# Gated recurrence of a two-block model: each level's exponents in two VectorE instructions, none of the stage's arithmetic on GpSimd

## The chip, the cores and the metric

One Trainium2 chip, one of its cores, one launch. The metric is the device time of the whole program in microseconds. The engines of the core are called by the names of the profile: PE (TensorE), ACT (ScalarE), DVE (VectorE), POOL (GpSimd), SP (SyncE, which issues most DMAs). Each engine takes its instructions in the order in which they stand in its queue.

## What is computed

Two blocks of a model on 512 tokens of width 1024. The first mixes tokens by a gated recurrence in both directions and by attention, and then has a mixture of 16 experts; the second has sparse attention, a short convolution and a feed-forward layer. The change lies in the recurrence of the first block, which has 4 heads of 128 channels:

```python
def hgrn_gates(f_pre, lb):
    f_pre = heads(f_pre.astype(jnp.float32), HG_HEADS)
    lb = lb.reshape(HG_HEADS, HG_DK)
    log_f = jnp.log(lb + (1 - lb) * jax.nn.sigmoid(f_pre))
    key = (1 - lb) * jax.nn.sigmoid(-f_pre)
    return key, log_f

def hgrn_chunk_scan(q, k, v, log_f, s0):
    """S_t = diag(f_t) S_{t-1} + k_t v_t^T, o_t = S_t^T q_t."""
    ...
        cum = jnp.cumsum(fc, axis=2)
        rel = jnp.where(incl, cum[:, :, :, None, :] - cum[:, :, None, :, :], -jnp.inf)
        scores = jnp.einsum("bhtk,bhsk,bhtsk->bhts", qc, kc, jnp.exp(rel))
    ...

def hgrn_bidir(q, i, k_f, lf_f, k_b, lf_b, s_f0, s_b0):
    o_f, s_f = hgrn_chunk_scan(q, k_f, i, lf_f, s_f0)
    flip = lambda a: a[:, ::-1]
    o_b, s_b = hgrn_chunk_scan(flip(q), flip(k_b), flip(i), flip(lf_b), s_b0)
    return o_f + flip(o_b), s_f, s_b
```

## The kernel before, in words

Channels lie on the partitions and the 512 tokens along the free axis. `first_mixer` runs `ctx_part` (the context's keys, values and states), then `hgrn` (the recurrence), `attention`, `merge_b`, `mix_out`, `router`, `moe`; then come `second_mixer` and `ffn`.

`hgrn` alternates two pieces of code for heads 0 to 3. `gates(h)` multiplies the activations by four blocks of 128 columns of the input weights (forget gates forward and backward, queries, output gate), 24 matmuls of 128x512 a block (L84 to L86, three for each 128 rows, since weights and activations are split into a high and a low part; ACT makes the high part at L76, DVE the low part at L78). It then takes a sigmoid (L564), a logarithm (L569) and the output gate `gr` (L572 to L575). `hgrn_head` takes the running sums of the logarithms in both directions (the scans of L610 and L611), subtracts the logarithm of the keys (L619), and then goes through seven levels, from blocks of 128 tokens down to blocks of 2 (L641 to L663). At each level the pairs of tokens that lie in the two halves of one block get their scores from one product: queries and keys are scaled by exponentials of the distance of their sums to the sum at the middle of the block. The tile `D` holds the exponents, `D[:, 0]` for queries and `D[:, 1]` for keys. L650 and L651 (DVE) write the query half, forward and backward direction apart, L652 and L653 (POOL) the key half; L654 (ACT) takes the exponential of both, L655 (DVE) multiplies by the queries, and L627 (PE) makes the scores, in `fs` for the two upper levels and in `lv` for the five lower ones, which DVE merges by a predicated copy (L663).

After the levels come the states: ACT makes the decayed keys (L675, L676), PE transposes them (`kt`, L685) and multiplies by the values (`sp`, L690), DVE chains the three states of a direction (`S`, L693) from the context's state, which POOL copies in at L678 and L679. PE then makes the head's output `po` (L702 to L704), ACT squares it (L708), PE sums over channels (`pr`, L711), and DVE and ACT apply the norm and the gate. Behind head 3, `hgrn` ends with twelve blocks of 24 matmuls of 128x256 that give keys, values and queries of the attention.

The program text doesn't give the order on the engines. A scheduler places all instructions by its own estimate of their times and keeps the data dependencies, so the matmuls of `gates(h + 1)` stand on PE in among those of `hgrn_head(h)`, and an instruction that takes another time in that estimate moves others. A tile's buffer is reused when everything that read its last contents is done (`D` has 4, `lv` 2, `S` and `Q` 1).

Of the kernel before, what the change touches and what calls it, by code (L numbers as in the profile page):

```python
# [13 lines left out]
AF = mybir.ActivationFunctionType  # L14
# [48 lines left out]

class Build:
# [26 lines left out]
    def wT(self, w, c0, n):  # L91
        """Yields (hi, lo) [128, 8, 128] for each 128 columns of w[:, c0:c0+n]."""
# [12 lines left out]
    def wN(self, w, c0, n):  # L105
        """Yields for each 256 columns the list over k of (hi, lo) [128, 256]."""
        w3 = w.rearrange("(k p) f -> p k f", p=128)
        K = w3.shape[1]
        for c in range(c0, c0 + n, 256):
            m = min(256, c0 + n - c)  # L110
            t = self.wload(w3[:, :, c:c + m], [128, K, m])
            ks = []
            for k in range(0, K, 4):
                h, l = self.split(t[:, k:k + 4, :], [128, 4, m])
                ks += [(h[:, i], l[:, i]) for i in range(4)]
            yield ks

    def gemmT(self, wh, wl, xh, xl, n0, n1):
        """out^T block: weights stationary, tokens n0:n1 moving."""
# [7 lines left out]
    def gemmN(self, ks, xh, xl, b, ps=None):  # L127
        """token block b of out: activations stationary, weights moving."""
# [9 lines left out]
    def rstd(self, pool, out, ss, scale, n):  # L138
        """out = 1/sqrt(ss*scale + eps) on [128, n]"""
# [38 lines left out]
    def first_mixer(self):  # L178
# [18 lines left out]
        at = 0  # L197
# [51 lines left out]
        # row statistics and transposes of x and ctx  # L249
# [25 lines left out]
        # scale and shift of the first norm by 256 columns, each pair followed by the activations' chunks  # L275
        wm3 = I["w_mod"][0].rearrange("(k p) f -> p k f", p=128)
        # mod[:, which, i, k]: shift (0), scale (1) for x (i=0) and ctx (i=1)
# [56 lines left out]
        def rest(i):  # L334
            """the last chunks of x, behind the first weights"""
# [68 lines left out]
    def ctx_part(self, cx, rest):  # L404
# [7 lines left out]
        # f gates of the context  # L412
# [8 lines left out]
        # shift and scale of the second norm by halves, each behind step i of what follows  # L421
# [9 lines left out]
        # i (values), tokens on partitions  # L431
# [8 lines left out]
        # keys and values of the attention: the context's  # L440
# [67 lines left out]
    def rope(self, pool, out, x, which, b, nh):  # L508
        """out = rope(x * gain): x [128, nh*64]"""
# [13 lines left out]
    def hgrn(self):  # L523
# [22 lines left out]
        def gates(h):  # L546
# [19 lines left out]
            # ln(key) stands in for key: it joins the exponents  # L566
# [4 lines left out]
            # gr / (1 + exp(-gr)); below -40, where the exponential nears the logarithm's bound, gr * exp(-40)  # L571
# [3 lines left out]
            nc.gpsimd.tensor_tensor(gr, sg, gr, op=ALU.mult)  # L575
# [7 lines left out]
        # keys, values and queries of the attention  # L583
# [12 lines left out]
    def table(self, name):  # L596
        """loads the activation tables of that name behind what was issued so far"""
        return self.tc.keep_in_program_order(self.nc.scalar.preload_act_table_set(name))

    def after(self, ins, first):  # L600
        """ins is issued behind first (the same engine)"""
# [4 lines left out]
    def hgrn_head(self, hp, pp, h, q, K, CU, sg):  # L606
# [5 lines left out]
        # P[s, t] for 4 blocks of 128 tokens; C holds its blocks of 32 on the diagonal  # L612
# [4 lines left out]
        nc.gpsimd.tensor_tensor(KS, kf, kb, op=ALU.add)  # L617
# [4 lines left out]
        def scores(out, kk, qq, m, x):  # L622
            """out[s, b, t'] for parts of m tokens: the part of t is that of s, x flipped"""
# [17 lines left out]
        for l in range(6, -1, -1):  # L641
# [4 lines left out]
            vw = lambda t: t.rearrange("p (n two h) -> p n two h", two=2, h=H)  # L646
            Dq, Dk, F, Bk, Fk, Bl = (vw(t) for t in (D[:, 0], D[:, 1], cf, cb, lf, lb))
            mf = F[:, :, 0, H - 1:H].to_broadcast([128, n, H])
            mb = Bk[:, :, 1, 0:1].to_broadcast([128, n, H])
            nc.vector.tensor_tensor(Dq[:, :, 1], F[:, :, 1], mf, op=ALU.subtract)  # L650
            nc.vector.tensor_tensor(Dq[:, :, 0], Bk[:, :, 0], mb, op=ALU.subtract)  # L651
            nc.gpsimd.tensor_tensor(Dk[:, :, 0], mf, Fk[:, :, 0], op=ALU.subtract)  # L652
            nc.gpsimd.tensor_tensor(Dk[:, :, 1], mb, Bl[:, :, 1], op=ALU.subtract)  # L653
# [14 lines left out]
        # chunk states  # L668
# [9 lines left out]
        nc.gpsimd.tensor_copy(S[:, 0, 0], self.S0[:, h, 0])  # L678
        nc.gpsimd.tensor_copy(S[:, 1, 3], self.S0[:, h, 1])  # L679
# [25 lines left out]
        # norm over the head's channels, gain, gate  # L705
# [13 lines left out]
    def attention(self):  # L719
# [4 lines left out]
        # keys: norm, rope, transpose, split; both halves of the partitions hold a copy  # L724
# [5 lines left out]
        # rope tables with the gains folded in: [which, block, cos|sin, 64]  # L730
# [32 lines left out]
        for n in range(2):  # L763
# [6 lines left out]
            # the norm of q and the softmax scale enter as the exponent's scale  # L770
# [54 lines left out]
    def gated(self, w_gate, c0, w_br, act, j, done):  # L825
        """done(j, sigmoid(gate block j), branch block j in PSUM) for two blocks of 128"""
# [42 lines left out]
    def mod_rows(self, pool, psp, wi, tag, halves=(0, 1)):  # L869
        """yields for halves of w_mod columns wi*1024..: rows 32j hold partial products of c"""  # L870
# [14 lines left out]
    def mod_bc(self, pool, psp, out, wi, tag, half):  # L885
        """a half of out [128, 1024]: that part of the modulation, the same on every partition; returns its end"""
# [13 lines left out]
    def mod_col(self, pool, psp, out, wi, half, tag="mr"):  # L900
        """half of out [128, 8]: that part of the modulation, by chunks of 128 on the partitions"""
# [10 lines left out]
    def mix_out(self, end):  # L912
        """X += g1 * y by groups of 256 columns, each followed into the router's logits"""
# [43 lines left out]
    def router(self):  # L957
        """aff: softmax of the logits; sl: the place (from 1) of a token among an expert's chosen, or 0"""
# [23 lines left out]
        # the 64 largest become -1  # L982
# [16 lines left out]
    def moe(self):  # L999
# [3 lines left out]
        # the first weights also fill places that are needed later  # L1003
# [6 lines left out]
        def mload(src, last):  # L1010
            if last == 2 and not self.tail:
                # the last product's: places that nothing else waits for
# [24 lines left out]
        def gemm_parts(ps, lhs, wa, wb):  # L1037
            """by parts of the columns"""
# [611 lines left out]
```

## Time and profile before

| | |
|---|---|
| median of three runs | 1845.2 us (1839.9 to 1847.11) |
| the profiled execution, first to last instruction | 1847.6 us |
| recurrence with the projections behind it, 131.0 to 330.5 us | 199.5 us |
| PE busy over the span | 1740.2 us (94%) |
| DVE busy over the span | 847.1 us (46%) |
| ACT busy over the span | 634.8 us (34%) |
| POOL busy over the span | 199.7 us (11%) |
| mean granted clock of PE | 0.969 |

The profiled execution is one more run than the three. Its record gives the span alone, 1847.6 us, which lies 2.4 us over the median. In the rows below, times are microseconds from the start of the span; a granted clock of 1.00 is 2.4 GHz and one of 0.50 is 1.2 GHz.

### The profile page before, as it was taken

The numbers are of one execution on the slowest core, as the hardware profiler recorded it, in microseconds if no ns is written. First come the engines' busy times: TensorE is split into PE (matmuls) and PEld (weight loads), VectorE is DVE, ScalarE is ACT, GpSimd is POOL, SyncE is SP. The second block draws the span as 40 slices with busy tenths as digits, with TensorE's granted clock in tenths as the row PEclk, the third lists the DMA queues.
The fourth block names the chain that finished last, engine by engine and source line by source line (L and its number), as shares of the span: only waits on it lengthen the run. The fifth ranks groups of instructions, "written<-read, shape, count | busy, mean of one in ns | idle before, by whom it ended". The sixth has DMA issues, their size and how long they took to land.

```text
span 1847.6 us, 27736 instructions
## 1 busy us (share of the span) xinstructions
PE 1740.2 (94%) x11511; PEld 1273.8 (69%) x11511; DVE 847.1 (46%) x1615; ACT 634.8 (34%) x1106; POOL 199.7 (11%) x231
## 2 busy tenths in 40 slices
PE   5998888999999599999999998899999999999999
PEld 2986668777778553444434433797677989898989
DVE  5637897865334512221221222656675553434342
ACT  4627674556333210010000100555463242313231
POOL 0103342122110000000000020500221000000000
PEclk9999898999999799999999999898899999999999
DMA  9562111201568578999999996341001222233231
GB/s 304 179 207 70 47 47 55 77 15 35 201 219 299 189 296 325 404 409 381 386 380 367 397 396 205 103 160 46 24 24 48 91 92 91 93 92 105 78 114 47
DMA packets 177398, 327.81 MB, mean 177 GB/s; under 512 B 8580, under 2 KB 115816, under 8 KB 177272
## 3 DMA queue, kind: packets, MB, share of 16 engines
q1 hardware_dynamic: 176480, 325.44, 49.0%
q8 instruction: 91, 1.49, 0.3%
q10 hardware_dynamic: 744, 0.51, 0.1%
q14 instruction: 35, 0.29, 0.1%
q0 software_dynamic: 48, 0.08, 0.0%
HBM read 323.91 MB, written 2.10 MB: 176 GB/s over the span
## 4 chain that ended last, share of the span: by engine, by line
PE 63%; DVE 4%; ACT 1%; issue 1%; DMA 1%; SPq 0%; ACTq 0%; DVEq 0%
PE mm L85 10%; PE mm L84 10%; PE mm L86 10%; PE G L1058 7%; PE U L1058 6%; PE Y L1058 5%; PE mm L1080 3%; PE po L1582 2%; PE mm L1153 1%; PE pt L1543 1%; PE sc L1522 1%; PE Y L1046 1%; PE mm L1154 1%; PE sc L1523 1%; PE hp L1445 0%
## 5 line engine op out<-in xcount | busy, mean ns | idle before, releaser
L76 ACT ACTIVATE whi<-wraw 128x1024 fp32r<-128x1024 f32 (+1 forms) x171 | 173.5, 1018 | 376.4 <-PE mm L85 177.9
L78 DVE TENSOR_TENSOR wlo<-wraw,whi 128x1024 fp32r<-128x1024 f32 (+1 forms) x171 | 207.2, 1213 | 125.7 <-ACT whi L76 125.3
L85 PE MATMUL mm<-whi,ul 128*128 128x256 f32 x512 | 144.3, 282 | 0.0
L86 PE MATMUL mm<-whi,uh 128*128 128x256 f32 x512 | 143.2, 281 | 0.0
L84 PE MATMUL mm<-wlo,uh 128*128 128x256 f32 x512 | 143.2, 281 | 0.0
L84 PE MATMUL mm<-HXl,whi 128*128 128x512 f32 x256 | 106.1, 415 | 0.0
L85 PE MATMUL mm<-HXh,wlo 128*128 128x512 f32 x256 | 105.9, 414 | 0.1
L86 PE MATMUL mm<-HXh,whi 128*128 128x512 f32 x256 | 105.2, 411 | 0.0
L84 PE MATMUL mm<-H,whi 128*128 128x512 f32 x256 | 99.7, 390 | 0.0
L85 PE MATMUL mm<-H,wlo 128*128 128x512 f32 x256 | 99.6, 389 | 0.0
L86 PE MATMUL mm<-H,whi 128*128 128x512 f32 x256 | 99.6, 389 | 0.0
L85 PEld LDWEIGHTS mm<-whi,ul 128*128 128x128 f32 x512 | 96.5, 188 | 1.0 <-DVE ul L1613 0.8
L84 PEld LDWEIGHTS mm<-wlo,uh 128*128 128x128 f32 x512 | 96.2, 188 | 0.2
L86 PEld LDWEIGHTS mm<-whi,uh 128*128 128x128 f32 x512 | 96.2, 188 | 0.0
L1080 PEld LDWEIGHTS mm<-D,X 128*128 128x128 f32 x512 | 61.9, 199 | 18.5 <-issue 15.4
L1622 DVE SCALAR_TENSOR_TENSOR X<-mm,r,X 128x256 f32<-128x256 f32 x64 | 30.9, 483 | 88.2 <-PE mm L86 88.2
L1080 PE MATMUL mm<-D,X 128*128 128x128 f32 x512 | 66.8, 288 | 2.8 <-DVE D L1075 1.8
L1146 POOL TENSOR_TENSOR X<-X,acc 128x1024 f32<-128x1024 f32 x4 | 9.3, 2369 | 534.7 <-issue 534.7
L1123 DVE TENSOR_TENSOR hy<-hy,U 128x1024 f32<-128x1024 f32 x8 | 9.8, 1222 | 124.4 <-PE U L1058 124.4
L1058 PE MATMUL Y<-mwt,xh 128*64 128x512 f32 x240 | 59.9, 594 | 5.4 <-DVE xh L1126 5.4
L1608 DVE TENSOR_SCALAR r<-mm 128x512 f32<-128x512 f32 x32 | 22.1, 691 | 85.2 <-PE mm L86 85.2
L1148 DVE SCALAR_TENSOR_TENSOR hy<-Y,gc,g 128x512 f32<-128x512 f32 (+1 forms) x17 | 11.6, 715 | 106.2 <-PE Y L1058 100.2
(541 smaller groups left out, 4238.9 us busy)
## 6 DMA issues: line engine op xcount, KB each, us to landing
mwt<-in_w_exp_gate_dram SPq DMA_DIRECT2D x41, 1024.0 KB, 8.3
mwt<-in_w_exp_up_dram SPq DMA_DIRECT2D x35, 1024.0 KB, 10.4
mwt<-in_w_exp_down_dram SPq DMA_DIRECT2D x33, 1024.0 KB, 11.9
wraw<-in_w_in_dram SPq DMA_DIRECT2D x29, 1024.0 KB, 5.3
wraw<-in_w_mod_dram SPq DMA_DIRECT2D x16, 1024.0 KB, 6.9
wraw<-in_w_up_dram SPq DMA_DIRECT2D x16, 1024.0 KB, 5.7
wraw<-in_w_down_dram SPq DMA_DIRECT2D x16, 1024.0 KB, 5.3
mwh<-in_w_exp_up_dram SPq DMA_DIRECT2D x30, 512.0 KB, 8.7
```

The lines of the kernel that those rows point to most:

```text
L76: i1 = self.nc.scalar.activation(hi, src, AF.Copy)
L78: i2 = self.nc.vector.tensor_tensor(lo, src, hi, op=ALU.subtract)
L84: mm(ps, ah, bl, start=first, stop=False)
L85: mm(ps, al, bh, start=False, stop=False)
L86: mm(ps, ah, bh, start=False, stop=last)
L1046: nc.tensor.matmul(y[64 * a:64 * a + 64], lhs[:, k, 64 * a:64 * a + 64], tl[a][k4], start=(k == 0), stop=(k == 7))
L1058: nc.tensor.matmul(ps[64 * a:64 * a + 64, n], lhs[:, k, 64 * a:64 * a + 64], tl[a][k2][:, n * 512:(n + 1) * 512], start=(k == 0), stop=(k ...
L1080: nc.tensor.matmul(ps, self.X[:, b, k * 128:(k + 1) * 128], Ds[:, b], start=(b == 0), stop=(b == 3))
L1153: nc.tensor.matmul(ps, oh[:, b * 128:(b + 1) * 128], yh[:, 1, s], start=True, stop=False)
L1582: nc.tensor.matmul(po[64 * j:64 * j + 64], lh, rh, start=(i == 0), stop=(i == len(items) - 1))
L1608: nc.vector.tensor_scalar(r, ps, 0.0, None, op0=ALU.max)
L1622: nc.vector.scalar_tensor_tensor(self.X[:, b, s], ps, r2[:, b:b + 1], self.X[:, b, s], op0=ALU.mult, op1=ALU.add)
```

## The change

The two DVE instructions of a level that write the query half become one, and the two POOL instructions that write the key half become one on DVE. A new helper `view` builds access patterns by hand: the new first axis of length 2 is the direction, and its step leads from the second half of a block in the forward sums to the first half in the backward sums (and the other way for keys). Besides, the product for `gr`, the sum of the keys `KS` move from POOL to DVE, and the two copies of the context's state move from POOL to ACT. The rest of the difference between the two programs is comments and docstrings, which are removed. Line numbers in the changed program are 5 higher up to the levels and 3 higher behind them.

```diff
+def view(t, at, dims):
+    return bass.AP(t.tensor, t.offset + at, [list(t.ap[0])] + dims)
...
-            nc.gpsimd.tensor_tensor(gr, sg, gr, op=ALU.mult)
+            nc.vector.tensor_tensor(gr, sg, gr, op=ALU.mult)
...
-        nc.gpsimd.tensor_tensor(KS, kf, kb, op=ALU.add)
+        nc.vector.tensor_tensor(KS, kf, kb, op=ALU.add)
...
             D = hp.tile([128, 2, 512], F32, name="D", tag="D", bufs=4)
-            vw = lambda t: t.rearrange("p (n two h) -> p n two h", two=2, h=H)
-            Dq, Dk, F, Bk, Fk, Bl = (vw(t) for t in (D[:, 0], D[:, 1], cf, cb, lf, lb))
-            mf = F[:, :, 0, H - 1:H].to_broadcast([128, n, H])
-            mb = Bk[:, :, 1, 0:1].to_broadcast([128, n, H])
-            nc.vector.tensor_tensor(Dq[:, :, 1], F[:, :, 1], mf, op=ALU.subtract)
-            nc.vector.tensor_tensor(Dq[:, :, 0], Bk[:, :, 0], mb, op=ALU.subtract)
-            nc.gpsimd.tensor_tensor(Dk[:, :, 0], mf, Fk[:, :, 0], op=ALU.subtract)
-            nc.gpsimd.tensor_tensor(Dk[:, :, 1], mb, Bl[:, :, 1], op=ALU.subtract)
+            late = lambda t: view(t, H, [[512 - H, 2], [B, n], [1, H]])
+            early = lambda t: view(t, 0, [[512 + H, 2], [B, n], [1, H]])
+            mid = view(CU, H - 1, [[513, 2], [B, n], [0, H]])
+            nc.vector.tensor_tensor(view(D, H, [[-H, 2], [B, n], [1, H]]), late(CU), mid, op=ALU.subtract)
+            nc.vector.tensor_tensor(view(D, 512, [[H, 2], [B, n], [1, H]]), mid, early(KL), op=ALU.subtract)
             nc.scalar.activation(D, D, AF.Exp)
...
-        nc.gpsimd.tensor_copy(S[:, 0, 0], self.S0[:, h, 0])
-        nc.gpsimd.tensor_copy(S[:, 1, 3], self.S0[:, h, 1])
+        nc.scalar.activation(S[:, 0, 0], self.S0[:, h, 0], AF.Copy)
+        nc.scalar.activation(S[:, 1, 3], self.S0[:, h, 1], AF.Copy)
```

The scheduler answers with another order, at two places above all. The first is PE in the lower levels of head 0. `lv<-D` and `fs<-D` are the scores of a level, `kt` and `sp` belong to the states, `po` to the head's output; `mm` are the products of the next head's gates. Before:

```order
L627 MATMUL lv<-D 32x32 x16
L86 MATMUL mm<-HXh,whi 128x512
L685 MATMUL kt<-ca,D 128x128
L84 MATMUL mm<-HXl,whi 128x512
L85 MATMUL mm<-HXh,wlo 128x512
L685 MATMUL kt<-ca,D 128x128
L86 MATMUL mm<-HXh,whi 128x512
L84 MATMUL mm<-HXl,whi 128x512
L85 MATMUL mm<-HXh,wlo 128x512
L627 MATMUL lv<-D 32x32 x16
L86 MATMUL mm<-HXh,whi 128x512
L690 MATMUL sp<-V,kn 128x128 x3
```

and now:

```order
L632 MATMUL lv<-D 32x32 x48
L688 MATMUL kt<-ca,D 128x128
L632 MATMUL lv<-D 32x32 x16
L688 MATMUL kt<-ca,D 128x128 x2
L693 MATMUL sp<-V,kn 128x128 x3
L632 MATMUL lv<-D 32x32 x16
L688 MATMUL kt<-ca,D 128x128 x3
L705 MATMUL po<-P,V 128x128
L706 MATMUL po<-Q,S 128x128
L693 MATMUL sp<-V,kn 128x128 x3
L89 MATMUL mm<-HXl,whi 128x512
```

Before, matmuls of the next head's gates stand between the levels down to the last: 30 of them from the first `fs<-D` of head 0 to its last `lv<-D`, 23 in head 1, 29 in head 2. Now there are 8 in head 0, 10 each in heads 1 and 2 and none in head 3; from the first `lv<-D` to the second `sp` not one is left, 16 stand between that and the rest of `po`, and the last three of the next head's second gate stand behind `pr`.

The second place is DVE at the end of head 0, where `D<-D,q` is the last levels' multiplication by the queries, `C` the merged lower levels, `S` the states and `wlo` the low part of a block of weights. Before:

```order
L78 TENSOR_TENSOR wlo<-wraw,whi 128x1024
L663 COPY_PREDICATED C<-lev,lv 128x128
L655 TENSOR_TENSOR D<-D,q 128x512
L78 TENSOR_TENSOR wlo<-wraw,whi 128x1024
L663 COPY_PREDICATED C<-lev,lv 128x128
L693 SCALAR_TENSOR_TENSOR S<-S,dec,sp 128x128
L666 COPY P<-C 32x4x32 x4
```

and now:

```order
L658 TENSOR_TENSOR D<-D,q 128x512
L561 TENSOR_SCALAR R<-mm 128x512
L696 SCALAR_TENSOR_TENSOR S<-S,dec,sp 128x128
L666 COPY_PREDICATED C<-lev,lv 128x128
L696 SCALAR_TENSOR_TENSOR S<-S,dec,sp 128x128
L669 COPY P<-C 32x4x32 x4
L696 SCALAR_TENSOR_TENSOR S<-S,dec,sp 128x128
L83 TENSOR_TENSOR wlo<-wraw,whi 128x1024
L696 SCALAR_TENSOR_TENSOR S<-S,dec,sp 128x128
L83 TENSOR_TENSOR wlo<-wraw,whi 128x1024
```

The low parts of the weights, which stood among the levels, now stand between the steps of the second direction's states, three of them there in all, and every head from 0 to 2 has this same order.

## Rows read from the trace of the kernel before

**Rows 1.** The page, part 1: busy time by engine.

```profile
span 1847.6 us, 27736 instructions
PE 1740.2 (94%) x11511; PEld 1273.8 (69%) x11511; DVE 847.1 (46%) x1615; ACT 634.8 (34%) x1106; POOL 199.7 (11%) x231
```

**Rows 2.** Busy time by stretch: from:to, length, busy (instructions), granted clock, DMA.

```profile
131.00:330.50 199.50, 178.24 (x1937) 146.29 (x1936) 162.22 (x285) 125.44 (x184) 72.87 (x81) 0.91 0.20 59
330.50:570.00 239.50, 235.80 (x1425) 178.58 (x1423) 126.76 (x244) 117.06 (x200) 45.08 (x44) 1.00 0.34 115
```

**Rows 3.** Timeline, DVE: the forward scan of each head (start, took, instruction, idle before).

```profile
149.85 1.23 DVE L610 TENSOR_TENSOR_SCAN R<-seg,R 128x512 f32<-128x512 f32 x1 [2.71 <-ACT R L569]
...
184.15 1.71 DVE L610 TENSOR_TENSOR_SCAN R<-seg,R 128x512 f32<-128x512 f32 x1 [0.78 <-ACT R L569]
...
231.87 1.23 DVE L610 TENSOR_TENSOR_SCAN R<-seg,R 128x512 f32<-128x512 f32 x1 [1.81 <-ACT R L569]
...
266.18 1.71 DVE L610 TENSOR_TENSOR_SCAN R<-seg,R 128x512 f32<-128x512 f32 x1 [0.78 <-ACT R L569]
```

**Rows 4.** Timeline, PE: the last two projections behind the recurrence.

```profile
330.23 0.28 PE L85 MATMUL mm<-whi,HXl 128*128 128x256 f32 x1
330.35 0.28 PE L86 MATMUL mm<-whi,HXh 128*128 128x256 f32 x1
```

**Rows 5.** Timeline of head 0's upper levels, DVE and, below, POOL.

```profile
155.72 0.85 DVE L650 TENSOR_TENSOR D<-R 128x256 f32<-128x256 f32 x1
156.50 0.85 DVE L651 TENSOR_TENSOR D<-R 128x256 f32<-128x256 f32 x1
...
155.48 0.81 POOL L652 TENSOR_TENSOR D<-R,KL 128x256 f32<-128x256 f32 x1
```

**Rows 6.** Timeline, DVE: head 0's lowest levels, POOL being done.

```profile
171.65 0.41 DVE L650 TENSOR_TENSOR D<-R 128x256 f32<-128x256 f32 x1
...
173.12 0.67 DVE L655 TENSOR_TENSOR D<-D,q 128x512 f32<-128x512 f32 x1
173.72 1.21 DVE L78 TENSOR_TENSOR wlo<-wraw,whi 128x1024 fp32r<-128x1024 f32 x1
174.85 0.29 DVE L663 COPY_PREDICATED C<-lev,lv 128x128 f32<-128x128 uint8 x1
175.05 0.68 DVE L655 TENSOR_TENSOR D<-D,q 128x512 f32<-128x512 f32 x1
```

**Rows 7.** Timeline, end of head 0: DVE, then ACT.

```profile
181.46 1.11 DVE L693 SCALAR_TENSOR_TENSOR S<-S,dec,sp 128x128 f32<-128x128 f32 x3
...
180.07 1.92 ACT L564 ACTIVATE R<-R 128x2048 f32<-128x2048 f32 x1
```

**Rows 8.** Timeline, end of head 1: DVE, PE, then ACT.

```profile
218.18 1.11 DVE L693 SCALAR_TENSOR_TENSOR S<-S,dec,sp 128x128 f32<-128x128 f32 x3 [1.14 <-PE sp L690]
...
222.04 0.60 ACT L708 ACTIVATE sq<-po 128x512 f32<-128x512 f32 x1 [7.33 <-PE po L704]
...
226.63 1.92 ACT L564 ACTIVATE R<-R 128x2048 f32<-128x2048 f32 x1
```

**Rows 9.** Timeline, PE: head 1's upper levels and the idle time before them.

```profile
196.23 0.69 PE L627 MATMUL fs<-D 128*64 128x64 f32 x16 [1.83 <-DVE D L655]
197.64 0.46 PE L627 MATMUL fs<-D 128*32 128x32 f32 x32 [0.72 <-DVE D L655]
...
201.88 0.66 PE L627 MATMUL lv<-D 128*32 128x32 f32 x32 [2.21 <-DVE D L655]
```

**Rows 10.** Busy time by stretch, as in rows 2: where the granted clock was halved.

```profile
160.50:167.30 6.80, 6.18 (x58) 4.50 (x59) 6.72 (x7) 3.56 (x5) 4.98 (x6) 0.50 0.01 4
...
198.00:208.30 10.30, 8.10 (x92) 5.53 (x79) 10.30 (x17) 6.77 (x11) 6.40 (x7) 0.50 0.01 2
...
242.40:249.20 6.80, 5.99 (x57) 4.05 (x58) 6.72 (x7) 3.44 (x5) 4.98 (x6) 0.50 0.00 1
...
280.00:290.20 10.20, 7.77 (x130) 6.80 (x120) 10.20 (x16) 7.41 (x13) 6.75 (x7) 0.50 0.01 2
```

## The prediction, before the changed kernel ran

> **What bounds the kernel now.** The page's first part comes first: PE is busy 94% of the span, DVE 46%, POOL 11% [rows 1], so a saving on DVE or POOL counts only where PE waits for it. The table of busy time by stretch then tells where that is: in the recurrence, from 131.0 to 330.5 us, PE is busy for 178.2 of 199.5 us, and DVE for 162.2, its densest long stretch; behind it, to 570 us, PE is busy for 235.8 of 239.5 us at full clock [rows 2]. So PE is the bound behind the recurrence, and what the recurrence gains or loses should arrive at the end one for one.
>
> Inside the stage I read the timeline by engine. The forward scans of the four heads start at 149.85, 184.15, 231.87 and 266.18 us [rows 3]: intervals of 34.3, 47.7 and 34.3 us, by turns, 116.3 us in all; from the last scan to the last projection at 330.35 [rows 4] it is another 64.2 us. The turns have a cause. In head 0, ACT takes the next head's sigmoid at 180.07, before DVE ends the states at 182.6 [rows 7]: the next gates were multiplied while the levels ran, and their work on ACT is hidden. In head 1 the states end at 219.3, `po` is squared at 222.04 and the sigmoid starts only at 226.63 [rows 8], so from the end of the states to the next scan at 231.87 there are 12.6 us in which the next head hangs on a chain of PE and ACT.
>
> **The change part by part.** *Query half.* Two DVE instructions of 0.41 us [rows 6] become one with 512 elements per partition. The nearest row with that count is the multiplication L655, which alone takes 0.67 us and lets the next start 0.60 us later (173.12 to 173.72) [rows 6]. Bounds: 0.41 us, as if the length were free, and 0.82, as if the parts still cost their two starts. I take 0.60, since type, operands in SBUF and count are the same.
>
> *Key half.* Two POOL instructions of 0.81 us [rows 5] leave, one of 0.60 comes to DVE, with the same bounds. Beside POOL the DVE instructions of the upper levels take 0.85 us, 0.78 apart, though the same kind takes 0.41 when POOL is idle [rows 5, 6]. This slowing goes. Seven levels then cost DVE 7 x 2 x 0.60 = 8.4 us a head where the query half alone cost between 14 x 0.41 = 5.7 and 14 x 0.78 = 10.9 us.
>
> *`KS` and `gr`.* 0.60 us each on DVE. `KS` stands before the scan, where DVE waited 2.71 us for ACT in head 0 and 0.8 to 1.8 in the others [rows 3], and is hidden there; `gr` stands among the levels and counts. The state copies, 128x128 on ACT, cost at most the 0.60 us of a 128x512 each [rows 8]; they stand behind the squaring of `po`, where ACT waits for `pr`. Nothing.
>
> *The levels of a head.* In the new order DVE has, from the forward scan to the last multiplication by queries, three instructions of 128x1024 or scans at 1.14 (spacing of L78, 173.72 to 174.85), four predicated copies at 0.20 (174.85 to 175.05) and 25 at 0.60 [rows 6]: 3.4 + 0.8 + 15.0 = 19.2, and I allow 1.0 us for waits on PE and ACT: **20.2 us**, against 25.9 before (149.85 to 175.73) in head 0 [rows 3, 6]. The saving is real, but two of the 128x1024 low parts that DVE made in that time have only moved behind the levels.
>
> *From there to the last state.* In the order: a copy of 0.60, the predicated copy 0.20, the four copies into `P` about 0.9 (an estimate, four short ones at 0.20 to 0.25), six state steps at about 0.26 (1.11 us for three with the last one's end [rows 7] gives 0.37 at most; I take between) and three low parts of 1.14: 6.7, with 0.2 for the first `lv`: **6.9 us**. Before it was 175.73 to 182.57, 6.8 us: no gain.
>
> *From the last state to the next scan.* Here the order decides. In every head the next gate's last products now stand behind `po` and `pr`, as in head 1 before, so every head has the 12.6 us of rows 8, and I add 0.4 because one split of weights and two state copies now stand ahead of the sigmoid on ACT: **13.0 us**. In heads 0 and 2 this was hidden.
>
> *Sum at full clock.* An interval is 20.2 + 6.9 + 13.0 = 40.1 us, three are 120.3 against 116.3: 4.0 us lost. Behind head 3 there is no next gate: 20.2 + 6.9 + 2.2 for `po`, then 229 of the 288 projections that stand behind it in the order at 0.12 us (330.23 to 330.35 [rows 4]), 27.5, and about 1 for `pr`: 57.8 against 64.2 us, 6.4 gained. Together 2.4 us gained.
>
> *PE's clock.* Four stretches of the stage ran at a granted clock of 0.50, for 6.8, 10.3, 6.8 and 10.2 us [rows 10]; each followed upper levels in which PE waited for DVE. The second came with no long pause: idle times of 1.83, 0.72 and 2.21 us with short products of the levels between them [rows 9]. In the new order PE has 8 or 10 gate matmuls in a head's levels where it had 23 to 30, and none from the first `lv` to the second `sp`, some 10 us of DVE's levels and then the tail. I expect the half clock in every head, later than now and just where the next gates, `po` and `pr` run, which are on the path. In the trace work went on at half clock for about 6 us after it had resumed (6.18 us busy in the first stretch [rows 10]); 6.2 us at half clock lose 3.1 us of work. Bounds: nothing, or the 10.3 us stretch, 5.1 us. I take 3.1 a head, 12.4 in all. What the four stretches cost before is already in the 180.5 us from the first scan to the last projection.
>
> The Trainium skill, on the page "TensorE: Matmul & The Clock Gate", section "HAM oscillation — how this bites in real kernels", names as its abstract rule that one long idle gap of PE must be avoided; by that rule alone the clock would stay up here, since no single gap of the new order should be long, and the sum would be the 2.4 us gained. The rows of head 1 do not agree with it: there gaps of at most 2.21 us were followed by 10.3 us at half clock.
>
> *Total.* -2.4 + 12.4 = 10.0 us slower. On the profiled execution's 1847.6 us that is 1857.6; its span lies 2.4 us above the median of the runs, so against 1845.2 us I say **1855 us**.
>
> **The rivals.** *Faster.* PE finishes the second gate of the next head in time, as in heads 0 and 2 before, and every head keeps an interval like theirs less the shorter levels: 34.3 - 5.7 = 28.6 us, three of them 85.8 against 116.3, 30 us gained, 1815 us. It decides at one point: whether the next head's sigmoid starts before the last state step. For it speaks that DVE's stage gets shorter; against it that PE cannot pass its own order, and three products of that gate stand behind `pr`. A weaker form, three intervals of 38 us (2.3 us gained) beside the last head's 6.4, gives 1836.5.
>
> *No change.* The clock does not fall in the critical part: 2.4 us gained, 1843 us. For it speaks the Trainium skill's rule above; against it head 1 as it ran before [rows 9, 10].
>
> *Slower still.* The clock stays down for the longer stretch in each head: 4 x 5.1 - 2.4 = 18 us, 1863 us; or a merged instruction costs its 0.82 us, 14 x 0.22 = 3.1 us a head, 12 us more than forecast, 1867 us.
>
> *The change does less than it says.* If the hand-made views kept DVE waiting on the tile as a whole, the levels would lose their overlap with ACT. The order shows the query half of the next level still standing ahead of the key half of this one, so this has little weight; it would end among the slower ones.
>
> **How the numbers follow.** About 9 us, 0.5%, is what a measurement of this kernel can tell from no change. The forecast gets 0.50, no clock loss 0.25, the slower case 0.15, the faster one 0.08, the last 0.02. The forecast's own range is 1848 to 1861 (clock price from 1.4 to 4.6 us a head). The range for 8 in 10 takes in the case without clock loss and most of the slower one: 1842 to 1865. Slower by more than 0.5%, that is above 1854.4: a little over half of the forecast, the slower cases, a share of the case without loss for what the new order costs behind the stage: 0.52. Faster: 0.09. Within: 0.39.
>
> **What would show it.** Right: merged instructions of 0.68 us with spacing 0.60 on DVE and no POOL in the stage; scans 40 to 44 us apart in all three intervals, no turns; the next head's sigmoid behind `pr`; four stretches at half clock, each covering `po`; the last scan to the last projection 58 to 62 us; PE's time behind the stage as before. Wrong: intervals under 38 us, a clock that stays at 1.00 from the second `sp` on, or a difference that arises behind 330 us.

## The result, and the profile of the changed kernel

The changed kernel takes **1853.4 us** (median of 12 runs, 1848.3 to 1859.8), the kernel before on the same chips 1844.1 us (12 runs, 1838.7 to 1852.3): a ratio of 1.0056, with a 95% interval of 1.0039 to 1.0073, 9.3 us slower. The forecast was 1855, with a range of 1842 to 1865.

The page's first part, and the busy time by stretch up to the last projection and behind it, as in [rows 1, 2]:

```profile
span 1856.8 us, 27629 instructions
PE 1743.8 (94%) x11511; PEld 1279.6 (69%) x11511; DVE 834.8 (45%) x1623; ACT 635.1 (34%) x1114; POOL 133.8 (7%) x159
```

```profile
131.00:341.50 210.50, 184.07 (x1951) 153.53 (x1950) 153.75 (x296) 126.31 (x190) 6.14 (x10) 0.88 0.20 58
341.50:581.00 239.50, 236.85 (x1420) 179.56 (x1418) 123.91 (x243) 116.03 (x200) 46.55 (x44) 0.99 0.34 115
```

In the stage POOL falls from 72.9 to 6.1 us and DVE from 162.2 to 153.8 although it took over POOL's work; the stage is 11 us longer all the same, and its mean clock 0.88 instead of 0.91. The loss stands in the distances of the forward scans, which answer to [rows 3] (timeline of DVE):

```profile
151.14 1.23 DVE L615 TENSOR_TENSOR_SCAN R<-seg,R 128x512 f32<-128x512 f32 x1 [1.86 <-ACT R L574]
...
194.70 1.23 DVE L615 TENSOR_TENSOR_SCAN R<-seg,R 128x512 f32<-128x512 f32 x1 [1.00 <-ACT R L574]
...
238.73 1.23 DVE L615 TENSOR_TENSOR_SCAN R<-seg,R 128x512 f32<-128x512 f32 x1 [1.00 <-ACT R L574]
...
282.91 1.23 DVE L615 TENSOR_TENSOR_SCAN R<-seg,R 128x512 f32<-128x512 f32 x1 [1.00 <-ACT R L574]
```

They are 43.6, 44.0 and 44.2 us apart, 131.8 in all against 116.3, without the turns of before. The last projection (timeline of PE, as in [rows 4]) ends 58.6 us after the last scan, against 64.5 us:

```profile
341.22 0.28 PE L91 MATMUL mm<-whi,HXh 128*128 128x256 f32 x1
```

So the stage ends 10.9 us later: 1.3 from the first scan's start, 15.4 from the distances, 5.9 back behind the last scan. The first term is no part of the change: that scan starts anywhere between 149.0 and 151.5 us in the profiles of this study. Behind the stage nothing is lost: the span is 9.2 us longer.

Head 0's end shows what the distance is made of (timeline of DVE, then of ACT, as in [rows 7, 8]):

```profile
170.14 0.68 DVE L658 TENSOR_TENSOR D<-D,q 128x512 f32<-128x512 f32 x1
...
176.54 0.35 DVE L696 SCALAR_TENSOR_TENSOR S<-S,dec,sp 128x128 f32<-128x128 f32 x1 [1.08 <-PE sp L693]
...
179.34 0.34 DVE L696 SCALAR_TENSOR_TENSOR S<-S,dec,sp 128x128 f32<-128x128 f32 x1
```

```profile
183.71 0.60 ACT L711 ACTIVATE sq<-po 128x512 f32<-128x512 f32 x1 [7.95 <-PE po L707]
...
185.52 0.69 ACT L715 ACTIVATE sq<-pr,eps 128x512 f32<-128x512 f32 x1 [0.82 <-PE pr L714]
...
186.78 0.58 ACT L560 ACTIVATE R<-mm 128x512 f32<-128x512 f32 x1
187.26 1.05 ACT L81 ACTIVATE whi<-wraw 128x1024 fp32r<-128x1024 f32 x1
188.21 0.62 ACT L719 ACTIVATE AHh<-o 128x512 fp32r<-128x512 f32 x1
188.85 1.28 ACT L569 ACT_TABLE_LOAD   x1
190.14 1.92 ACT L569 ACTIVATE R<-R 128x2048 f32<-128x2048 f32 x1
```

The levels end at 170.82, 19.7 us after the scan, where they took 25.9. The last state is ready at 179.68, 8.9 us later; and only 10.5 us behind that does ACT take the next sigmoid, behind `sq` and the copy of the second gate. Before, in heads 0 and 2, the sigmoid ran ahead of the last state.

The clock was halved in four stretches of the stage, as in [rows 10]. This is busy time by stretch; the first row is the one ahead of the first half-clock stretch:

```profile
158.00:165.40 7.40, 4.82 (x123) 3.14 (x121) 7.40 (x15) 6.08 (x9) 0.00 (x0) 1.00 0.01 3
165.40:179.10 13.70, 10.58 (x125) 8.48 (x126) 11.69 (x24) 6.80 (x13) 0.00 (x0) 0.50 0.18 53
...
209.80:223.40 13.60, 11.09 (x126) 8.89 (x127) 11.58 (x24) 6.51 (x12) 0.00 (x0) 0.50 0.20 56
254.20:267.80 13.60, 11.46 (x127) 9.16 (x128) 11.27 (x24) 6.22 (x12) 0.00 (x0) 0.50 0.24 79
295.10:305.40 10.30, 6.27 (x142) 5.05 (x143) 9.54 (x20) 6.24 (x12) 0.00 (x0) 0.50 0.03 8
```

That is 51.2 us at the lower of the two levels against 34.1 before. In head 0 PE was busy for 4.82 of 7.40 us while the two upper levels and the first of the lower ones ran, and then the clock fell.

### The profile page after: what moved, and what is told of

It reads as the page before. It is cut to its first block, busy times and chain, and to the rows that moved or that the text cites. A ratio compares the mean times of both kernels' runs of the same rounds, so it can differ in the third digit from the quotient of the medians.

```text
span 1856.8 us, 27629 instructions
## 1 busy us (share of the span) xinstructions
PE 1743.8 (94%) x11511; PEld 1279.6 (69%) x11511; DVE 834.8 (45%) x1623; ACT 635.1 (34%) x1114; POOL 133.8 (7%) x159
## 4 chain that ended last, share of the span: by engine, by line
PE 63%; DVE 4%; ACT 1%; issue 1%; DMA 0%; SPq 0%; ACTq 0%; DVEq 0%
PE mm L90 10%; PE mm L89 10%; PE mm L91 10%; PE G L1061 7%; PE U L1061 6%; PE Y L1061 5%; PE mm L1083 3%; PE po L1585 2%; PE mm L1156 1%; PE pt L1546 1%; PE sc L1525 1%; PE Y L1049 1%; PE mm L1157 1%; PE sc L1526 1%; PE hp L1448 0%
## 5 line engine op out<-in xcount | busy, mean ns | idle before, releaser
L1083 PEld LDWEIGHTS mm<-D,X 128*128 128x128 f32 x512 | 62.1, 200 | 18.5 <-issue 15.4
L89 PEld LDWEIGHTS mm<-HXl,whi 128*128 128x128 f32 x256 | 49.9, 195 | 12.8 <-issue 2.6
## 6 DMA issues: line engine op xcount, KB each, us to landing
mwt<-in_w_exp_up_dram SPq DMA_DIRECT2D x35, 1024.0 KB, 10.5
```

The lines of the kernel that those rows point to most:

```text
L89: mm(ps, ah, bl, start=first, stop=False)
L1083: nc.tensor.matmul(ps, self.X[:, b, k * 128:(k + 1) * 128], Ds[:, b], start=(b == 0), stop=(b == 3))
```

## The experiments

The theory: the exponents without GpSimd are a gain; the loss comes from the order that the scheduler builds with them (few gate products among the levels, so that the next sigmoid stands behind `po` and `sq` in every head) and from the half clock that follows the sparse stretch. The rivals: VectorE's new load costs; the small moved steps cost; the clock has no part. The table has one row for each kernel, without the repeated runs; "to state" is from the last multiplication by `q` to the last state, "to scan" from there to the next forward scan (heads 0 to 2, from the timelines of VectorE), "end" the end of the last projection, "half clock" the time up to that end at a granted clock of 0.50. These columns come from one profiled execution, the time from the median; each ratio is to the kernel before on the same chip, and the kernels ran on several chips.

| kernel | distances of scans | levels | to state | to scan | end | half clock | time, us | ratio to before (95%) |
|---|---|---|---|---|---|---|---|---|
| before | 34.3, 47.7, 34.3 | 25.9–26.7 | 6.8–8.5 | 1.6, 12.6, 1.6 | 330.6 | 34.1 | 1844.1 | 1 |
| changed | 43.6, 44.0, 44.2 | 19.7–19.9 | 8.9 | 15.0–15.4 | 341.5 | 51.2 | 1853.4 | 1.0056 (1.0039–1.0073) |
| hold_before | 52.4, 51.8, 51.6 | 25.1 | 7.3–7.9 | 19.1–19.4 | 367.3 | 78.5 | 1881.0 | 1.0199 (1.0169–1.0228) |
| rest_only | 45.1, 44.7, 44.6 | 23.1–23.2 | 8.8–9.2 | 12.7 | 347.9 | 58.0 | 1862.9 | 1.0103 (1.0073–1.0132) |
| fill_after | 40.7, 40.8, 40.8 | 19.6–19.8 | 7.1 | 13.9 | 331.9 | 3.4 | 1844.1 | 1.0010 (0.9988–1.0032) |
| merge_only | 44.4, 44.4, 44.4 | 20.2 | 8.9 | 15.3–15.4 | 345.0 | 54.6 | 1853.2 | 1.0064 (1.0036–1.0091) |
| split_dve | 42.4, 41.7, 43.0 | 20.4 | 8.5–9.7 | 12.8 | 336.9 | 44.4 | 1850.5 | 1.0034 (1.0016–1.0053) |
| query_merge | 41.1, 46.5, 37.4 | 25.0–26.9 | 7.3–9.7 | 4.5, 11.7, 4.5 | 344.1 | 44.4 | 1847.2 | 1.0034 (1.0015–1.0053) |
| spread_before | 36.0, 39.6, 40.8 | 27.1–29.5 | 7.0–9.3 | 1.9–2.0 | 331.3 | 20.5 | 1845.8 | 1.0003 (0.9984–1.0023) |
| spread_after | 32.9, 33.6, 33.5 | 22.4–23.0 | 9.5 | 1.0 | 312.5 | 13.7 | 1822.5 | 0.9881 (0.9852–0.9910) |
| spread_all | 31.5, 33.5, 33.5 | 21.0–23.0 | 9.5 | 1.0 | 307.2 | 3.4 | 1818.0 | 0.9871 (0.9833–0.9908) |

### The order, with the exponents as they were: hold_before and rest_only

hold_before is the kernel before with the gates' products written out one triple at a time, so that each can be bound on PE (`self.last_sp` is the last product of the states so far):

```diff
+                        if h and (n or k > 2):
+                            self.after(i, self.last_sp)
```

> The arithmetic and the engines of the kernel before; in heads 1 to 3 the gate products beyond the first nine are held back on PE until the second three states' products of the head before, so that the sigmoid stands behind po in every head, as it does in the changed kernel. Theory (the order makes the loss): heads 0 and 2 lose the 34.3 us distance and take that of head 1 or more, 47 to 51 us in all three, time 1866 to 1882. Rival (where VectorE's and GpSimd's instructions run makes the loss, not PE's order): the sum of the distances stays near 116 us, time 1840 to 1850.

Measured 1881.0 us. ACT's timeline at the end of head 0:

```profile
186.73 0.60 ACT L713 ACTIVATE sq<-po 128x512 f32<-128x512 f32 x1 [5.86 <-PE po L709]
...
197.66 1.92 ACT L569 ACTIVATE R<-R 128x2048 f32<-128x2048 f32 x1
```

With the exponents untouched, the order with the sigmoid behind `sq` costs 37 us; the distances reach 52 us, a little over what was expected, since here the products of more than a whole gate stand behind `po`. More of the stage ran at half clock too (78.5 us against 34.1), but these stretches ended with the states (in head 0 at 183.0 us, the last state at 183.8), and levels and states together take 32.4 to 33.0 us where head 0 took 32.7 before: what is lost lies behind the states, at full clock.

rest_only is the kernel before with the four lines on `KS`, `gr` and the states' copies taken from the change, and no other:

> The kernel before with only the small steps of the change: the sum of the keys and the gate's last product on VectorE, the two copies of the first states on ScalarE; the exponents stay as they were, two on VectorE and two on GpSimd per level. The instructions' order comes out with the sigmoid behind sq in every head, though the exponents are untouched. Theory (that order is what loses): the 34.3 us distances of heads 0 and 2 become 46 to 51, time 1862 to 1880. Rival (the small steps matter little and the order of the sigmoid less): 1840 to 1850.

Measured 1862.9 us, 1.0103 (1.0073 to 1.0132). This is the change without its exponents, and it is slower than the whole change: the small edits are enough to turn the order. The distances, 44.6 to 45.1, lie 1 to 6 us under the expected ones, which were taken from the 47.7 of head 1: from the last state to the next scan it is 12.7 us as in head 1 before (12.6), but levels and states together take 31.9 to 32.4 us where head 1 took 35.1. The levels themselves shortened to 23.2 us with GpSimd still at work, since the two low parts of weights that stood among them in heads 0 and 2 (1.14 us each) stand behind them now.

### The clock alone: fill_after

The changed kernel, with products of the activations that nothing reads, bound in order behind the five lower levels' scores:

```diff
+        def fill(last, n):
+            for _ in range(n):
+                i = nc.tensor.matmul(idle, self.HX[0][:, 0, 0:128], self.HX[0][:, 1], start=True, stop=True)
+                self.after(i, last)
+                last = i
...
-                scores(small(ps), D[:, 1], D[:, 0], 32, 0)
+                fill(scores(small(ps), D[:, 1], D[:, 0], 32, 0), (2, 4, 1, 9, 3)[l])
```

> The changed kernel with 19 extra 128x512 products per head, whose result nothing reads, behind the scores of the five lower levels in each head; they use the same splits of the activations and stand where PE waited at half clock. Theory A (half clock is worth some 3 us of each of the four heads, as the sum of the prediction has it): the stretches at half clock shrink or go, the distances between scans fall from 43.6 to 44.2 us to about 40.5, and the time is 1841 to 1847. Theory B (order alone; the clock falls on work that was waiting anyway): the distances stay at 43 to 45 us and the time at 1851 to 1857. If the products are themselves in the way: above 1860.

Measured 1844.1 us, 9.3 under the changed kernel (on another chip; by the two ratios to before it is 8.5, by the distances of the scans 9.5), with 76 matmuls more. Busy time by stretch, where the changed kernel's three long half-clock stretches were, and the one that is left:

```profile
165.40:179.10 13.70, 12.36 (x155) 9.61 (x155) 12.02 (x25) 6.72 (x13) 0.00 (x0) 1.00 0.26 72
206.00:220.00 14.00, 12.64 (x157) 9.81 (x156) 12.25 (x26) 7.04 (x13) 0.00 (x0) 1.00 0.23 65
247.00:261.00 14.00, 12.66 (x158) 9.90 (x157) 12.05 (x25) 6.85 (x13) 0.00 (x0) 1.00 0.27 87
285.50:289.50 4.00, 4.00 (x42) 2.98 (x41) 3.93 (x9) 2.23 (x3) 0.00 (x0) 0.57 0.00 0
```

Theory A holds: up to the last scan VectorE, ScalarE and, but for the added products, PE have the changed kernel's order, the clock is up, and the distances fall by 2.9, 3.2 and 3.4 us. The last head gains nothing (58.65 us behind the last scan against 58.59). What the kernel before, with its own 34.1 us at half clock, would gain from such products was not measured.

### The parts of the change: merge_only, split_dve, query_merge

merge_only is the changed kernel with those four lines as they were before.

> The changed kernel with the small steps left where they were: the sum of the keys, the gate's last product and the two copies of the first states on GpSimd; the exponents are merged and on VectorE. The sigmoid stands behind sq in every head, as in the changed kernel. Theory (the small steps have cover; the loss comes with the order that the merged exponents bring): scans 43 to 45 us apart, time 1849 to 1857. Rival (the small steps on VectorE and ScalarE are what the changed kernel pays for): 4 us per head less, time 1836 to 1845.

Measured 1853.2 us, the changed kernel's time: beside the merged exponents the small steps are free on either engine.

split_dve splits both merged instructions again, on VectorE:

```diff
-            nc.vector.tensor_tensor(view(D, H, [[-H, 2], [B, n], [1, H]]), late(CU), mid, op=ALU.subtract)
-            nc.vector.tensor_tensor(view(D, 512, [[H, 2], [B, n], [1, H]]), mid, early(KL), op=ALU.subtract)
+            nc.vector.tensor_tensor(Dq[:, :, 1], F[:, :, 1], mf, op=ALU.subtract)
+            nc.vector.tensor_tensor(Dq[:, :, 0], Bk[:, :, 0], mb, op=ALU.subtract)
+            nc.vector.tensor_tensor(Dk[:, :, 0], mf, Fk[:, :, 0], op=ALU.subtract)
+            nc.vector.tensor_tensor(Dk[:, :, 1], mb, Bl[:, :, 1], op=ALU.subtract)
```

> The changed kernel with its two merged instructions per level split again into two of 256 columns each, all four on VectorE; nothing else differs, and the next head's sigmoid stands behind sq in every head as in the changed kernel. Theory (a merged instruction takes 0.60 us of VectorE where two take 0.82, and the levels are paced by VectorE): 0.44 us per level, 3.1 us per head, so scans 46 to 48 us apart and a time of 1863 to 1870. Rival (something else paces the levels, PE at half clock above all): within 3 us of the changed kernel's 1853.

Measured 1850.5 us: the expectation was wrong, and the rival right in the time, though not in its reason: VectorE is busy for 20.38 of the 20.41 us of head 0's levels, so nothing else paces them. The levels take 20.4 us, 0.5 to 0.7 more than merged, not 3.1. VectorE's timeline in the lower levels of head 2 says why:

```profile
247.38 0.42 DVE L662 TENSOR_TENSOR D<-R,KL 128x256 f32<-128x256 f32 x1
247.71 0.42 DVE L659 TENSOR_TENSOR D<-R 128x256 f32<-128x256 f32 x1
248.05 0.42 DVE L660 TENSOR_TENSOR D<-R 128x256 f32<-128x256 f32 x1
248.38 0.29 DVE L672 COPY_PREDICATED C<-lev,lv 128x128 f32<-128x128 uint8 x1
```

An instruction of 256 columns lasts 0.42 us, but the next one starts 0.33 to 0.34 us after it. Two occupy the engine for 0.67 us, not 0.82, so a merge spares 0.07 us. So it is not the halved number of instructions that shortened the levels. Of the 5.5 us between the 25.9 of before and these 20.4, rest_only has 2.7 already, with GpSimd at work: mostly the low parts that moved. The other 2.8 us come as the exponents leave GpSimd (one copy of 0.60 us moved behind the levels as well). That the distances, 41.7 to 43.0 us, are even shorter than the changed kernel's is the order on ACT: from `sq` to the sigmoid it takes 4.9 us here (181.88 to 186.76) against 6.4.

query_merge merges only the queries' pair; the keys' pair and the small steps stay on GpSimd, and the sigmoid stands ahead of `sq` in heads 0 and 2, as before.

> The kernel before with the queries' two exponent instructions merged into one on VectorE; the keys' two stay on GpSimd, and the small steps too. The order keeps the sigmoid ahead of sq in heads 0 and 2 and behind it in head 1, as in the kernel before. Theory (the merge is a gain, and only the lost order a loss): levels some 2 to 4 us shorter than the 25.9 us of before, GpSimd's pair setting the pace; heads 0 and 2 keep distances of 32 to 35 us, head 1 falls from 47.7 to 44 to 46; time 1834 to 1843. Rival (merged instructions on VectorE cost by themselves or by contention with GpSimd): 1846 or more.

Measured 1847.2 us, 1.0034 (1.0015 to 1.0053). The theory's gain did not come. The groups of instructions of VectorE (columns: busy us, mean ns of one, idle before), and the timelines of VectorE and of GpSimd among the levels of head 3:

```profile
L663 DVE TENSOR_TENSOR D<-D,q 128x512 f32<-128x512 f32 x28 | 31.7, 1148 | 1.1 <-ACT D L662 1.1
L655 DVE TENSOR_TENSOR D<-R 128x512 f32<-128x512 f32 x28 | 28.1, 1015 | 0.1
```

```profile
290.01 1.15 DVE L663 TENSOR_TENSOR D<-D,q 128x512 f32<-128x512 f32 x1
291.09 1.22 DVE L655 TENSOR_TENSOR D<-R 128x512 f32<-128x512 f32 x1
292.23 1.21 DVE L663 TENSOR_TENSOR D<-D,q 128x512 f32<-128x512 f32 x1
...
289.51 1.11 POOL L661 TENSOR_TENSOR D<-R,KL 128x256 f32<-128x256 f32 x1
290.58 1.18 POOL L660 TENSOR_TENSOR D<-R,KL 128x256 f32<-128x256 f32 x1
291.72 1.17 POOL L661 TENSOR_TENSOR D<-R,KL 128x256 f32<-128x256 f32 x1
```

The same two groups in the changed kernel, with GpSimd empty:

```profile
L658 DVE TENSOR_TENSOR D<-D,q 128x512 f32<-128x512 f32 x28 | 19.2, 687 | 0.3 <-ACT D L657 0.3
L655 DVE TENSOR_TENSOR D<-R 128x512 f32<-128x512 f32 x28 | 19.2, 685 | 0.1
```

Beside GpSimd the merged instruction takes 1.02 us in the mean instead of 0.69 and the multiplication 1.15 instead of 0.69, and GpSimd's own, 0.81 us in [rows 5], take 1.11 to 1.18 here. The two engines start by turns, 290.01, 290.58, 291.09, 291.72, 292.23, so that each of them starts every 1.1 us: of a VectorE instruction that would let the next start after 0.60 us, the rest is GpSimd's turn. The levels are as long as before, and the sigmoid, now just before `sq`, leaves 4.5 us to the next scan instead of 1.6. Since the profiled execution lay 9.6 us above its median, it ran once more:

> query_merge once more, since its profiled execution lay 9.6 us above its own median. If its distances of 41.1, 46.5 and 37.4 us belong to that execution alone, by the half clock falling elsewhere, this one shows 34 to 38 us for heads 0 and 2; if they belong to the kernel, the same distances come again. Time 1844 to 1850 either way.

It gave 1851.2 us, 1.0059 (1.0035 to 1.0082), a little more than the 1844 to 1850 expected, with levels of 25.0 to 25.6, the same 4.5 us, and distances of 36.3, 46.5 and 38.9. Neither case fits whole. The first distance fell by 4.8 us, 3.0 of them between levels and last state, and head 0 had 6.8 us at half clock where it had 13.6: that much belonged to the one execution. The third did not come under 38. In both executions heads 0 and 2 stay above the 34.3 us of before; what part of that is half clock was not measured.

### The order made for the change: spread_before, spread_after, spread_all

Sixteen of the next head's 32 gate triples are bound between the levels' scores (5 behind the scores of `KS`, then two behind each of the upper levels and 1, 3, 1, 2, 0 behind the lower ones):

```diff
+        def between(last, n):
+            for p in itertools.islice(parts, n):
+                self.after(p[0], last)
+                self.held = [p[1]]
...
-                scores(small(ps), D[:, 1], D[:, 0], 32, 0)
+                between(scores(small(ps), D[:, 1], D[:, 0], 32, 0), (0, 2, 1, 3, 1)[l])
```

> The change's arithmetic, nothing left out; only PE's order is bound: 16 of the next head's 32 gate triples (three 128x512 products each) stand between the levels' scores, in heads 0 to 2. Theory (the change loses by the order alone: too few gate products among the levels, so that the next head's sigmoid stands behind po and sq, and the sparse stretch runs at half clock): the sigmoid comes before sq in all three heads, the stretch at half clock shrinks to some us per head or goes, the distances between forward scans fall from 43.6 to 44.2 us to 33 to 36, and the time is about 1826 (1818 to 1836), under both kernels. Rival (VectorE is the bound now that everything is on it): distances stay above 41 us, time 1845 to 1855.

Measured 1822.5 us, 0.9881 (0.9852 to 0.9910), and 1820.8 us, 0.9887 (0.9860 to 0.9915), when run again: 31 us under the changed kernel, 22 under the one before. Full clock in the changed kernel's order gave 9.3 of these 31 (fill_after), so the order is worth some 22. The timelines of VectorE and, below, of ACT at the end of head 0:

```profile
182.12 0.34 DVE L716 SCALAR_TENSOR_TENSOR S<-S,dec,sp 128x128 f32<-128x128 f32 x1
182.38 0.48 DVE L583 TENSOR_SCALAR R<-R,oml 128x512 f32<-128x512 f32 x1
182.90 0.69 DVE L633 TENSOR_TENSOR KS<-R 128x512 f32<-128x512 f32 x1
183.51 1.22 DVE L626 TENSOR_TENSOR_SCAN R<-seg,R 128x512 f32<-128x512 f32 x1
...
178.47 1.92 ACT L579 ACTIVATE R<-R 128x2048 f32<-128x2048 f32 x1
```

From the last state to the next scan VectorE does not wait any more. A head takes 33.5 us, and in head 1 VectorE is busy for 31.9 of them and PE for 33.3; which of the two sets the pace was not tested. The half clock is gone from heads 1 and 2 (busy time by stretch, the levels of head 1):

```profile
196.00:206.00 10.00, 10.00 (x206) 7.15 (x202) 9.98 (x20) 7.81 (x13) 0.00 (x0) 1.00 0.01 2
```

spread_before has the same binding with the engines of before:

> The arithmetic and the engines of the kernel before (two instructions of a kind per level, the keys' on GpSimd), with the same 16 gate triples bound between the levels' scores as in spread_after. Theory (the merged instructions are worth some 5 us of a head's levels, hidden by the order): slower than spread_after by 4 to 6 us per distance between scans, 12 to 18 us in all, so 1838 to 1844 if spread_after gives 1826; the distances are 38 to 41 us in all three heads. Rival (the merge gives nothing by itself; contention of VectorE and GpSimd is hidden anyway): within 4 us of spread_after.

Measured 1845.8 us: 23 us more than spread_after, more than the 12 to 18 expected; the first distance, 36.0 us, came under the expected 38 to 41, the other two within. The levels beside GpSimd grew to 27.1 to 29.5 us in heads 0 to 2: three low parts stand among them, and in heads 1 and 2 the output of the head before, up to three of its instructions at 1.11 to 1.16 us. So with this binding the change is worth 23 us; in the order that the scheduler gave it, it loses 9.

spread_all treats the last head in the same way, with the key and value projections:

> spread_after with the last head treated in the same way: the key and value projections (32 triples of 128x256 products) stand between the last head's levels, where spread_after has PE waiting for 5 us between 262 and 272 us and at half clock from 267 to 277.5 us. Theory: the waits of PE and the half clock of the last head go, 4 to 9 us; time 1813 to 1819, the last scan to the last projection 53 to 58 us instead of 61.7. Rival (what follows the last state is bound by VectorE and ScalarE, whose copies out of PSUM now stand among the levels): no gain, 1820 to 1828.

> spread_after once more, beside spread_all on one chip, to tell the two apart: 1820 to 1825.

> spread_all once more, beside spread_after on one chip. If the 4.7 us by which its stage after the last scan was shorter (57.2 against 61.9 us) last to the end: 3 to 6 us under spread_after. If what follows the stage takes them up (the projections' consumers wait for something else): within 2 us of it.

The stage behind the last scan took 57.2 us against 61.9. The times were 1818.0 and, beside spread_after's 1820.8 on one chip, 1815.3 us, 0.9862 (0.9833 to 0.9892). Both differences, 4.5 us (on two chips; 1.8 by the ratios to before) and 5.5 on the same one, point the same way, but the intervals overlap; the gain is likely and not settled. It is the fastest version of the study.

## Why the prediction was right, step by step

- **Merged instructions.** 0.60 us apart, as taken; the group's mean is 0.685. The upper bound of 0.82 was too high, because it added durations where the engine's rhythm is the distance of starts, and so was the rival at 1867 us that stood on it.
- **The levels.** They take 19.7 to 19.9 us against the 20.2 forecast, for the reasons given: two low parts moved behind (2.3 us), and the slowing beside POOL went (2 to 3 us, rest_only against split_dve). The merge itself gave 0.5 to 0.7 us. Of the 1.0 us allowed for waits next to nothing came: VectorE was busy for 19.6 of the 19.7 us of head 0's levels.
- **`KS` and the copies at nothing, `gr` at 0.60 us among the levels.** Right in the sum (merge_only has the same time). Their part in the order was not foreseen: rest_only shows that they turn it alone.
- **From the last multiplication to the last state.** 6.9 forecast; 7.1 at full clock in fill_after, 8.9 in the changed kernel, of which 1.7 to 1.8 us is thus clock.
- **From there to the next scan.** 13.0 was too small: 13.9 at full clock, 15.0 to 15.4 as it ran. From `sq` to the sigmoid ACT needs 6.4 us (183.71 to 190.14, and as long in fill_after) where it needed 4.6 in head 1 before [rows 8]. The forecast added 0.4 for a split of weights and two state copies, but a split stood there before too; ACT's timeline of head 1 before:

```profile
222.53 1.05 ACT L76 ACTIVATE whi<-wraw 128x1024 fp32r<-128x1024 f32 x1
223.48 0.59 ACT L555 ACTIVATE R<-mm 128x512 f32<-128x512 f32 x1
223.96 0.69 ACT L712 ACTIVATE sq<-pr,eps 128x512 f32<-128x512 f32 x1
```

  The split and the gate's copy filled the wait for `pr` there. Now they stand behind it (ACT waits 0.82 us), and the copy of the output, `AHh`, which came after the sigmoid, stands ahead of it.
- **An interval at full clock.** 40.1 forecast, 40.7 to 40.8 in fill_after. Behind the last scan 57.8 forecast, 58.65. The 2.4 us to be gained come out as 0: fill_after to before is 1.0010 (0.9988 to 1.0032).
- **The half clock.** 12.4 us forecast; 9.3 us by the times of fill_after. Right in kind: it fell in every head though the largest gap of PE in head 0's levels was 2.34 us, and at the fall, at 165.4 us, PE had waited for only 1.0 us of it. The timeline of PE in head 0, now and, below, before:

```profile
166.75 0.66 PE L632 MATMUL lv<-D 128*32 128x32 f32 x32 [2.34 <-DVE D L658]
...
161.12 1.12 PE L627 MATMUL fs<-D 128*64 128x64 f32 x16 [3.91 <-DVE D L655]
```

  By the Trainium skill ("TensorE: Matmul & The Clock Gate", "HAM oscillation — how this bites in real kernels") the long gap is what must be avoided. Heads 0 and 2 before agree with it: the clock fell there in pauses of 3.91 and 3.62 us. The changed kernel does not, nor does head 1 before, where the clock fell at 198.0 us behind pauses of 1.83 and 0.72 us; the one of 2.21 us, which the prediction counts among those ahead of it, came after the fall. So avoiding the long gap was not enough here. The place was wrong: I put the stretches over `po`. They came earlier, over the lower levels, the states and the gate products between (165.4 to 179.1 in head 0), and the rest of `po` ran at full clock. By fill_after the first three heads lost 2.9 to 3.4 us each and the last none, where 3.1 had been put on each of the four.
- **The total.** 10.0 forecast, 9.3 measured. So close a number is luck, since two errors nearly cancel: about 2 us too little in the three distances at full clock and 0.9 behind the last scan, some 3 us too much on the clock. The parts that did hold are the order's loss behind the states and a half clock in every head.

Of the rivals, *no change* is what fill_after shows, and *faster* what spread_after shows: its point of decision, the sigmoid ahead of the last state step, is met there (178.47, the last state step starting at 182.12), and the time is 1822 and not 1815, because levels and states together take 31.9 to 32.5 us in that order, with the next head's copies and, from head 1 on, the output of the head before among them, where I had reckoned with the shorter levels alone: the distances are 32.9 to 33.6 us and not 28.6.

PE's time behind the stage was as before, as the text said. The scans were to be 40 to 44 us apart and the last projection 58 to 62 us behind the last scan; they are 43.6 to 44.2 apart, and it is 58.6.

## What to carry to other kernels

An edit on an engine that is not the bound can be a gain in its own stretch and a loss in the sum, if a scheduler builds another order with it: compare what stands before the next stage's first input in both orders, and if the edit empties an engine, bind the filling work there by hand. Price instructions that follow each other by the distance of their starts, not by their durations. Before merging two instructions to save starts, look whether a neighbour on another engine slows them; here taking the exponents off that neighbour was worth 2 to 3 us of a head's levels and the merge some half a microsecond.

## What was not expected of the hardware

- In query_merge VectorE and GpSimd take turns at instructions with two inputs from SBUF, whole instructions at a time: a 128x512 f32 one on VectorE, which takes 0.69 us with GpSimd empty, takes 1.15 beside it, GpSimd's 128x256 one 0.81 us beside VectorE's short instructions and 1.11 to 1.18 beside the long ones. The Trainium skill ("SBUF — State Buffer", section "SBUF: two separate sides") calls the ports that the two share an exclusive lock, held for a whole instruction; the alternating starts of query_merge agree with it. So a longer merged instruction on one of the two also holds up the other, which the expectation of query_merge had left out.
- 19 extra matmuls a head made the kernel faster: with them PE was busy for 12.4 of 13.7 us at a granted clock of 1.00 where it had been busy for 10.6 at 0.50, and the kernel took 9.3 us less.
